# Hyena short convolution in a two-layer encoder kernel: shifted products by ScalarE activations and accumulating DMAs in place of VectorE

## Chip, cores and metric

The kernel runs on one core of one Trainium2 chip. The metric is device time in microseconds (us) of one execution. The core's engines are PE (TensorE; its weight loads are listed apart as PEld), DVE (VectorE), ACT (ScalarE), POOL (GpSimd) and SP (SyncE, which only issues DMAs here). POOL issues DMAs too.

## Reference

A trunk of two layers on 1024 tokens of 1024 channels, all in float32. Layer 0 mixes tokens by attention and RWKV-7, layer 1 by a bidirectional Hyena operator, and each layer ends with a gated feed-forward network. The change lies in the Hyena operator:

```
p = h @ w_in                                        # [1024, 3 * 1024]
p = conv_general_dilated(p, conv_w, width 3, centred, one filter per channel) + conv_b
v, x1, x2 = jnp.split(p, 3, axis=-1)
z = v
for o, gate in enumerate((x1, x2)):
    z = gate * bidirectional_fft_conv(z, filt[:, o, 0], filt[:, o, 1], skip[o])
return z @ w_out
```

The width-3 convolution is, for each channel, `w0 * p[t-1] + w1 * p[t] + w2 * p[t+1] + b`.

## The kernel before, in words

Channels lie on the 128 partitions and tokens along the free dimension. SBUF is cut into pages of 128 x 1024 float32 (called p in the profile), PSUM into eight banks of 128 x 512 (bk). Pages and banks are taken and given back while the program is written down, the oldest free one first, so taking a page means waiting for its last users.

The Hyena layer runs two chains side by side.

The **front** (`front`, `finish`) makes 24 tiles of 128 channels, in four pieces of six: two tiles of v, two of x1, two of x2. For each tile `proj_steps` multiplies by weights that POOL's queue loads one tile ahead (`load_w`, L271, two DMAs of 512 KB from the DRAM tiles hwi..., into pages that the tile before the last has to release): 48 products of 128x512 on PE (L296, float32 as pairs of two parts) into two banks. `padded` (L1033 to L1036) copies the banks to a page with a zero column at each end; POOL sets the zeros and ACT copies. `hy_short` then makes the convolution: ACT writes o = w1 * pad[1:1025] + b (L1818), DVE adds w0 * pad[0:1024] (L1819) and w2 * pad[2:1026] (L1820). For v and x1 `hy_tok` transposes o on PE (L1831) and ACT copies the transposes out (L1832); x2 is stored to DRAM by SP (sp_h).

The **back** (`back`) takes the pieces in turn. `start` makes the first transform of v on PE (L1770, "sums"), and ACT evicts it (L1771). `hy_conv` is a long run of DVE work: a transform (`dft8`, L1648 and L1649), products with the filters' spectra (L1794 to L1798, spectra loaded by SP, L1793), sums (L1804, L1805) and a transform back. `gate` then multiplies back on PE (L1923), DVE multiplies by x1 (L1928), and PE makes the next transform (L1780, "taps"), evicted by ACT (L1698) and combined by DVE (L1699, L1700). A second `hy_conv` follows, with the sums of the next piece inside it, and `finals` (PE L1946, DVE L1950) ends the piece. Behind the front's last tile the output projection of the first four results (`tail`, L296 and L787) runs beside the back.

`weave` puts the two chains into one program in proportion to given costs, and the framework's scheduler then sets each engine's order. An engine works through its order one by one, so an instruction that waits holds up all behind it.

Of the kernel before, what the change touches and what calls it, by code (L numbers as in the profile page):

```python
# [32 lines left out]
def rows(ap):  # L33
    """[n*128] (or [a, n*128]) vector -> [rows, 128]."""
    if len(ap.shape) == 2:
        return ap.rearrange("a (r w) -> (a r) w", w=P)
    return ap.rearrange("(r w) -> r w", w=P)
# [9 lines left out]
def weave(*gens):  # L47
    """Runs generators of steps side by side, in proportion to their lengths: (n, generator). A step counts for what it
    yields, or for one; one that yields "wait" has to wait for the others."""
# [19 lines left out]
def some(gen, n):  # L69
    """The next n steps of a generator."""  # L70
    for _ in range(n):
        if next(gen, gen) is gen:
            return
        yield


class Kern:
    """The kernel's shared state and building blocks.

    SBUF is cut into pages and PSUM into banks, handed out and taken back while the program is traced: the oldest  # L80
    free one first, so that reuse waits as little as it can. Pages are for float32 ([128, 1040]) or for float32r
    operands of products ([128, 1024]); repage() cuts the free ones anew between the parts of the program.
    """

# [32 lines left out]
    def fence(self, dt, n=1 << 30, first=0):  # L117
        """Only the pages from `first` up to the n-th are for common use."""
# [11 lines left out]
    def repage(self, nf, nr):  # L130
        """Cuts the pages into nf of float32 and nr of float32r; those in use stay."""
# [36 lines left out]
    def set_banks(self, *counts):  # L168
        """Splits the (free) banks into groups."""
# [23 lines left out]
    def small(self, tag, shape, bufs, dt=F32):  # L193
        """One of `bufs` small tiles in turn; the caller sees to it that an older use has ended by then."""
# [20 lines left out]
    def load_cols(self, spec):  # L215
        """spec: list of (key, AP [rows, width] or tuple of APs set side by side); a row becomes a column. Steps of 128."""
# [42 lines left out]
    def split(self, t, shape=(P, 1024)):  # L259
        """The pair of a page, which is given back."""  # L260
        hi, lo = self.page(shape, F32R), self.page(shape, F32R)
        self.split_into(hi, lo, t)
        self.free(t)
        return hi, lo

    def load_w(self, ap, kt, ncol):
        """ap: DRAM [kt*128, ncol] -> (hi, lo), [128, kt, ncol] each; ap may also be what presplit() returned."""
# [9 lines left out]
    def presplit(self, ap, kt, ncol, name):  # L277
        """The pair of load_w() as DRAM tiles."""
# [7 lines left out]
    def mm3(self, ps, w, mov, first=True, last=True, halves=(0, 1)):  # L286
        """ps[n] = sum_k w[k]^T mov[k][:, n-th half]; pairs (hi, lo) of [128, M] and [128, 1024]. The first and last
        addends may be left to other calls."""
# [9 lines left out]
    def proj_steps(self, w, c0, width, h, g=0, ahead=None, n=4, apart=False):  # L298
        """proj_tile() in n steps; the halves one after the other if `apart`."""
# [15 lines left out]
    def stream(self, w, h, tiles, g=0):  # L315
        """Projections one after another, each one's `post` beside the next: (column, width, post), post(banks) a generator."""
        late = iter(())
        n = 4
# [17 lines left out]
    def proj_tile(self, w, c0, width, h, g=0, ahead=None):  # L336
        """w[:, c0:c0+width]^T h in two banks; a column in `ahead` is that of the next call, whose weights are loaded here."""
# [33 lines left out]
    def ada_first(self):  # L371
        """Layer 0's first two sixths, by the tensor engine."""
# [19 lines left out]
    def ada_cols(self, layer, part, half, acc, g):  # L392
        """The columns of half a sixth from rows to be summed."""
# [13 lines left out]
    def ada_part(self, layer, part, g=0, lag=0):  # L407
        """Modulation columns of one sixth: [128, 8] at self.mod[:, layer*48 + part*8]. The last product of a half comes
        `lag` steps after its sums."""
# [35 lines left out]
    def rstd(self, acc, n):  # L445
        """1/sqrt(mean_D(x^2) + eps) on all partitions, [128, 512] of a half in PSUM; acc holds sums of squares."""
# [12 lines left out]
    def normed(self, xT, steps, use, lag, keep=None):  # L459
        """use(n, m, r) for the halves n of the tiles m of x, r the bank of rstd(); `steps` yields (n, m) as they get done,  # L460
        half 0 first. A tile that is done goes to the tile `keep` in DRAM. Half 0 is used beside the steps of half 1, from
        its step `lag` on."""
# [31 lines left out]
    def inv_sqrt(self, out, ps, mult, add=None, floor=None):  # L494
        """out = 1/sqrt(ps*mult + add) or 1/sqrt(max(ps, floor))."""
# [8 lines left out]
    def norm_h(self, xT, layer, which, steps, lag, keep=None):  # L504
        """rmsnorm(x)*gain*(1+scale)+shift as pairs of [128 channels, 1024 tokens]; for the rest see normed()."""
# [23 lines left out]
    def head_cols(self, sq, g):  # L529
        """sq [128 = 2 heads x 64, 1024 tokens] -> bank [128 tokens, 8 blocks, 2 heads] of sums."""  # L530
# [5 lines left out]
    def head_bcast(self, cols, n, g):  # L536
        """cols [128 tokens, 8, 2 heads] -> bank [128 = 2 heads x 64, 512] of token half n."""
# [7 lines left out]
    def to_tok(self, out, src, g):  # L545
        """src [128 channels, 1024 tokens] -> out [128 tokens, 8 blocks, 128 channels]."""
# [9 lines left out]
    # The up-projections multiply blocks of 2 x 2 (two tiles of outputs, halves of the channels, halves of the tokens)  # L556
    # with seven products, Winograd's form of Strassen's: with C = A B,
# [1619 lines left out]
```

## Time and profile before

| | us |
|---|---|
| median of 3 timed runs | 3468.43 |
| lowest and highest of them | 3458.44, 3473.36 |
| span of the profiled execution, which is one by itself | 3477.4 |
| Hyena layer in it, first L1818 to the end of the last L1950 | 2187.1 to 2736.6 |

The profiled execution's own time is known as its span, from the first instruction to the last. Busy time of an engine is the time in which it worked on an instruction; a timeline merges instructions of one line and gives start, length, count, and in square brackets the idle time ahead with what ended it. Times in timelines and stretches count from the start of the span.

### The profile page before, as it was taken

The page shows a single profiled execution, that of the slowest core. Times are in us where ns is not written, and L with a number is a line of the kernel's source. Part 1 is how long each engine was busy: PE and PEld are TensorE (multiplying, and loading weights), DVE is VectorE, ACT ScalarE, POOL GpSimd, SP SyncE. Part 2 cuts the span into 40 slices and gives each one's busy share as a digit, 9 for nine tenths or more (in the row PEclk, how much of TensorE's full clock was granted, in tenths as well). Part 3 has the DMA queues.
Part 4 walks back from the last instruction along what each step waited for, and adds up shares of the span by engine and source line. Part 5 has one row for each costly group of instructions (what it writes and reads, how often), then busy time and mean ns, then how long its engine had stood idle before and what let it go on. Part 6 is the DMA issues. An engine that isn't in the chain of part 4 may idle for free.

```text
span 3477.4 us, 52810 instructions
## 1 busy us (share of the span) xinstructions
PE 3277.4 (94%) x20739; PEld 2639.1 (76%) x20739; DVE 2355.9 (68%) x4281; ACT 1255.1 (36%) x2296; POOL 240.6 (7%) x502
## 2 busy tenths in 40 slices
PE   8999989999998998999999999989987799999998
PEld 4577766777677887887788887778876688888887
DVE  5345556566667778587777666589987786667545
ACT  4523245556543543342223333321221153333211
POOL 2000000000011231000000220000000000000000
PEclk9789989999998999999999999999998899999999
DMA  7454523333324326234444994324336523223411
GB/s 261 172 164 148 159 84 75 73 96 82 73 63 105 99 77 213 79 127 151 158 147 135 359 356 160 103 81 144 121 104 228 177 74 108 73 73 129 146 53 49
DMA packets 332536, 458.89 MB, mean 132 GB/s; under 512 B 103992, under 2 KB 234897, under 8 KB 332288
## 3 DMA queue, kind: packets, MB, share of 16 engines
q1 hardware_dynamic: 292576, 321.65, 30.1%
q0 software_dynamic: 39536, 133.81, 11.3%
q8 instruction: 163, 2.67, 0.3%
q14 instruction: 85, 0.70, 0.1%
q10 hardware_dynamic: 176, 0.07, 0.0%
HBM read 311.27 MB, written 141.56 MB: 130 GB/s over the span
## 4 chain that ended last, share of the span: by engine, by line
PE 60%; DVE 9%; DMA 5%; issue 4%; ACT 2%; SPq 0%; POOL 0%; DVEq 0%; ACTq 0%; POOLq 0%
PE bk L296 22%; PE bk L600 7%; PE bk L602 7%; PE bk L601 7%; PE bk L1749 4%; PE bk L1735 2%; PE bk L1770 2%; DMA p<-in_ada_w_dram 2%; DVE p L1648 1%; DVE p L257 1%; PE bk L1263 1%; PE bk L1327 1%; PE bk L947 1%; DMA p<-in_hy_w_in_dram 1%; PE bk L964 1%
## 5 line engine op out<-in xcount | busy, mean ns | idle before, releaser
L296 PE MATMUL bk<-p,p 128*128 128x512 f32 (+1 forms) x5136 | 1252.3, 403 | 66.9 <-ACT p L256 26.4
L296 PEld LDWEIGHTS bk<-p,p 128*128 128x128 f32 (+1 forms) x5136 | 979.5, 193 | 304.4 <-ACT p L256 30.1
L256 ACT ACTIVATE p<-p 128x512 fp32r<-128x512 f32 (+3 forms) x534 | 395.8, 759 | 930.3 <-PE bk L601 260.6
L257 DVE TENSOR_TENSOR p<-p,p 128x512 fp32r<-128x512 f32 (+3 forms) x534 | 443.5, 848 | 225.3 <-ACT p L256 183.6
L601 PE MATMUL bk<-p,p 128*128 128x512 f32 x1248 | 488.3, 392 | 3.8 <-DVE p L257 3.8
L600 PE MATMUL bk<-p,p 128*128 128x512 f32 x1248 | 488.4, 393 | 0.0
L602 PE MATMUL bk<-p,p 128*128 128x512 f32 x1248 | 487.6, 392 | 0.2 <-DVE p L257 0.2
L601 PEld LDWEIGHTS bk<-p,p 128*128 128x128 f32 x1248 | 236.3, 189 | 53.4 <-DVE p L257 4.7
L602 PEld LDWEIGHTS bk<-p,p 128*128 128x128 f32 x1248 | 236.2, 189 | 50.4 <-DVE p L257 0.8
L600 PEld LDWEIGHTS bk<-p,p 128*128 128x128 f32 x1248 | 236.1, 189 | 48.9
L787 DVE SCALAR_TENSOR_TENSOR p<-bk,mod,p 128x512 f32<-128x512 f32 x192 | 135.0, 745 | 119.8 <-PE bk L296 116.6
L1648 DVE TENSOR_TENSOR p<-p 128x128 f32<-128x128 f32 (+2 forms) x544 | 174.0, 383 | 0.0
L429 DVE SCALAR_TENSOR_TENSOR p<-p,cond,p 128x512 f32<-128x512 f32 x140 | 104.5, 748 | 82.7 <-DMA p<-in_ada_w_dram 81.0
L1749 PE MATMUL bk<-p,p 128*128 128x128 f32 x1024 | 137.0, 290 | 2.7 <-DVE p L1700 2.6
L1749 PEld LDWEIGHTS bk<-p,p 128*128 128x128 f32 x1024 | 126.5, 201 | 7.9 <-ACT p L1737 2.4
L928 DVE TENSOR_REDUCE mx<-bk 128x1 f32<-128x512 f32 x128 | 86.9, 685 | 61.8 <-PE bk L925 58.8
L1737 ACT ACTIVATE p<-delta,k_tneg 128x128 f32<-128x128 f32 x256 | 87.9, 394 | 84.0 <-DMA hs<-p 14.0
L1036 ACT COPY p<-bk 128x512 f32<-128x512 f32 (+1 forms) x80 | 44.0, 589 | 197.3 <-DVE p L1797 64.3
L948 ACT COPY p<-bk 128x512 f32<-128x512 f32 x128 | 74.4, 588 | 105.3 <-PE bk L947 100.7
L932 ACT ACTIVATE p<-bk,mx 128x512 f32<-128x512 f32 x128 | 87.0, 686 | 29.4 <-DVE mx L929 29.0
L947 PE MATMUL bk<-k_ident,p 128*128 128x128 f32 x512 | 85.0, 294 | 10.8 <-ACT p L932 9.3
L1327 PEld LDWEIGHTS bk<-p,p 64*64 64x64 f32 x2048 | 73.0, 137 | 28.9 <-issue 17.6
(404 smaller groups left out, 4373.4 us busy)
## 6 DMA issues: line engine op xcount, KB each, us to landing
p<-in_ffn_w_dram SPq DMA_DIRECT2D x120, 512.0 KB, 4.5
p<-in_ada_w_dram SPq DMA_DIRECT2D x96, 512.0 KB, 4.5
sp_f<-p POOLq DMA_DIRECT2D x36, 512.0 KB, 5.5
p<-sp_f POOLq DMA_DIRECT2D x36, 512.0 KB, 5.4
hs<-p POOLq DMA_DIRECT2D x64, 256.0 KB, 3.1
p<-hs SPq DMA_DIRECT2D x32, 512.0 KB, 4.2
p<-sp_r SPq DMA_DIRECT2D x24, 512.0 KB, 5.6
p<-sp_x SPq DMA_DIRECT2D x24, 512.0 KB, 4.5
```

Of the source, the lines that this page charges most:

```text
L256: self.nc.scalar.activation(out=hi, in_=src, func=AF.Copy)
L257: self.nc.vector.tensor_tensor(out=lo, in0=src, in1=hi.bitcast(F32), op=ALU.subtract)
L296: nc.tensor.matmul(ps[n], a, b[:, HALVES[n]], start=s, stop=e)
L429: nc.vector.scalar_tensor_tensor(out=acc, in0=wt[:, i], scalar=self.cond[:, k : k + 1], in1=acc, op0=ALU.mult, op1=ALU.add)
L600: nc.tensor.matmul(ps, op[:, 0, k], mh, start=start and k == 0, stop=False)
L601: nc.tensor.matmul(ps, op[:, 0, k], ml, start=False, stop=False)
L602: nc.tensor.matmul(ps, op[:, 1, k], mh, start=False, stop=stop and k == 3)
L787: nc.vector.scalar_tensor_tensor(out=xs, in0=ps[n], scalar=self.modc(layer, part, m), in1=xs, op0=ALU.mult, op1=ALU.add)
L947: nc.tensor.transpose(pt[:, j], pr[:, k * P : (k + 1) * P], self.ident)
L1327: nc.tensor.matmul(pt[H[p], pr], lhs(e, pr, p), rhs[H[p], 8 * e + pr], start=True, stop=True)
L1648: tt = lambda o, a, b, op: nc.vector.tensor_tensor(out=o, in0=a, in1=b, op=op)
L1749: nc.tensor.matmul(ps[:, j, ri], F[2 * d + t2 // 4][:, t2 % 4, 128 * ri : 128 * ri + 128], tp[:, j, d], start=d == 0, stop=d == 1)
```

## The change

ACT makes all three scaled copies, into three pages. POOL then issues two DMAs from page to page that add to what the destination holds: first the copy scaled by w0 into o, then the copy scaled by w2. A tile takes two pages more, each for a short while. Only `hy_short` differs; other lines move by four numbers (L1831 becomes L1835, L1923 L1927, L1946 L1950).

```diff
     def hy_short(self, pad, j):
         nc = self.nc
-        o = self.page()
+        o, a = self.page(), self.page()
         cw = lambda a: self.c("conv_w", 24 * a + j)
         nc.scalar.activation(out=o, in_=pad[:, 1:1025], func=AF.Identity, scale=cw(1), bias=self.c("conv_b", j))
-        nc.vector.scalar_tensor_tensor(out=o, in0=pad[:, 0:1024], scalar=cw(0), in1=o, op0=ALU.mult, op1=ALU.add)
-        nc.vector.scalar_tensor_tensor(out=o, in0=pad[:, 2:1026], scalar=cw(2), in1=o, op0=ALU.mult, op1=ALU.add)
-        self.free(pad)
+        nc.scalar.activation(out=a, in_=pad[:, 0:1024], func=AF.Identity, scale=cw(0))
+        nc.gpsimd.dma_start(out=o, in_=a, accum_op=ALU.add)
+        self.free(a)
+        a = self.page()
+        nc.scalar.activation(out=a, in_=pad[:, 2:1026], func=AF.Identity, scale=cw(2))
+        nc.gpsimd.dma_start(out=o, in_=a, accum_op=ALU.add)
+        self.free(a, pad)
         return o
```

The scheduler's orders differ from the first tile on. Three places show how. In all of them p_ and a number is a page, bk_ a bank.

POOL at the start of the layer, before: loads of weights (hwi), one pair of DMAs for each tile, with one pad's zero column between them.

```order
L271 DMA p_238<-hwi8h 128x1024
L271 DMA p_11467<-hwi8l 128x1024
L271 DMA p_11455<-hwi9h 128x1024
L271 DMA p_11483<-hwi9l 128x1024
L1034 MEMSET p_86 128x1
L271 DMA p_238<-hwi16h 128x1024
L271 DMA p_11467<-hwi16l 128x1024
```

POOL at the same place with the change, from the load of hwi9 on:

```order
L271 DMA p_11483<-hwi9l 128x1024
L1820 DMA p_106<-p_94 128x1024
L1034 MEMSET p_86 128x1
L1820 DMA p_90<-p_16650 128x1024
L1824 DMA p_106<-p_102 128x1024
L1824 DMA p_90<-p_16654 128x1024
L271 DMA p_238<-hwi16h 128x1024
L271 DMA p_11467<-hwi16l 128x1024
L1033 MEMSET p_106 128x1
L1820 DMA p_16662<-p_16666 128x1024
L1824 DMA p_16662<-p_16670 128x1024
L271 DMA p_11455<-hwi17h 128x1024
```

The weight loads and the pads' zeros now stand behind the accumulating DMAs of earlier tiles, and each L1824 has to wait for the L1820 into the same page.

ACT at the first two tiles, before: pad copies, one activation for each tile, then copies of transposes.

```order
L1036 COPY p_86<-bk_66 128x512
L1036 COPY p_94<-bk_68 128x512
L1818 ACTIVATE p_106<-p_86,cols 128x1024
L1818 ACTIVATE p_130<-p_94,cols 128x1024
L1832 COPY p_102<-bk_69 128x4x128
```

ACT at the same place with the change:

```order
L1036 COPY p_86<-bk_66 128x512
L1036 COPY p_98<-bk_68 128x512
L1818 ACTIVATE p_106<-p_86,cols 128x1024
L1819 ACTIVATE p_94<-p_86,cols 128x1024
L1823 ACTIVATE p_102<-p_86,cols 128x1024
L1818 ACTIVATE p_90<-p_98,cols 128x1024
L1819 ACTIVATE p_16650<-p_98,cols 128x1024
L1823 ACTIVATE p_16654<-p_98,cols 128x1024
L1036 COPY p_16658<-bk_63 128x512
```

Each tile has three activations in a row, and the copies of transposes come after the next tile's pad copies.

PE inside the first gate, before (L1923 gate products, L1780 taps, L296 projection products):

```order
L1780 MATMUL bk_64<-p_94,p_122 128x256 x2
L1923 MATMUL bk_70<-p_130,p_118 128x256 x2
L1923 MATMUL bk_70<-p_130,p_126 128x256 x2
L296 MATMUL bk_66<-p_11495,p_11467 128x512
L1923 MATMUL bk_67<-p_16654,p_118 128x256 x2
L1923 MATMUL bk_67<-p_16654,p_126 128x256 x2
L1780 MATMUL bk_64<-p_94,p_122 128x256 x2
```

PE inside the first gate with the change:

```order
L1780 MATMUL bk_64<-p_90,p_122 128x256 x2
L1927 MATMUL bk_70<-p_16678,p_118 128x256 x2
L1927 MATMUL bk_70<-p_16678,p_126 128x256 x2
L296 MATMUL bk_68<-p_11491,p_11455 128x512
L296 MATMUL bk_69<-p_242,p_11455 128x512
L296 MATMUL bk_68<-p_242,p_11455 128x512
L296 MATMUL bk_69<-p_11491,p_11483 128x512
L296 MATMUL bk_68<-p_11491,p_11483 128x512
L296 MATMUL bk_69<-p_11475,p_11455 128x512
L296 MATMUL bk_68<-p_11475,p_11455 128x512
L1927 MATMUL bk_67<-p_16698,p_118 128x256 x2
```

More projection products stand inside the gate. Over the first gate there are 78 of them where there were 50, over the third none where there were 24, and over the fourth 109 where there were 81. Counted from the first product of the third tile, 286, 600, 912 and 1128 projection products stood ahead of the four gates, and 246, 542, 912 and 1056 stand there now; 1272 stand ahead of the end of the last piece in both. Of the transposes of the first two tiles the change's order puts both behind the 48 products of the third tile, where they stood behind 29 and 72.

## Rows read from the trace of the kernel before

**Rows 1.** Page, part 1: engine, busy us (share of the span), instructions.
```profile
PE 3277.4 (94%) x20739; PEld 2639.1 (76%) x20739; DVE 2355.9 (68%) x4281; ACT 1255.1 (36%) x2296; POOL 240.6 (7%) x502
```
**Rows 2.** Stretches of the Hyena layer: busy time of each engine in each.
```profile
core 0: us, PE busy (x) PEld busy (x) DVE busy (x) ACT busy (x) POOL busy (x), PEclk, DMA share, GB/s
2216.00:2600.00 384.00, 354.25 (x1656) 298.11 (x1655) 338.33 (x591) 87.67 (x133) 22.94 (x65) 0.96 0.33 108
...
2276.00:2400.00 124.00, 113.92 (x535) 96.13 (x534) 108.98 (x183) 26.74 (x40) 8.52 (x25) 0.94 0.36 119
2400.00:2520.00 120.00, 113.35 (x541) 95.93 (x540) 112.32 (x200) 25.21 (x38) 7.26 (x21) 0.97 0.35 114
2520.00:2645.00 125.00, 97.33 (x445) 79.92 (x444) 113.81 (x195) 26.82 (x39) 6.87 (x17) 0.89 0.43 146
2645.00:2737.00 92.00, 66.35 (x282) 54.93 (x281) 69.55 (x128) 4.35 (x6) 4.25 (x8) 0.83 0.61 207
```
**Rows 3.** PE timeline: third tile's start, a run of projection products, the four gates' first products.
```profile
2191.58 8.48 PE L296 MATMUL bk<-p,p 128*128 128x512 f32 x29 [4.99 <-DMA p<-hwi8h]
...
2250.72 25.23 PE L296 MATMUL bk<-p,p 128*128 128x512 f32 x110
2275.78 1.89 PE L1923 MATMUL bk<-p,p 128*128 128x256 f32 x8
...
2400.39 1.89 PE L1923 MATMUL bk<-p,p 128*128 128x256 f32 x8
...
2520.12 1.89 PE L1923 MATMUL bk<-p,p 128*128 128x256 f32 x8
...
2644.56 1.89 PE L1923 MATMUL bk<-p,p 128*128 128x256 f32 x8
```
**Rows 4.** DVE timeline: the last piece's gated products.
```profile
2732.21 4.37 DVE L1950 TENSOR_TENSOR p<-p,bk 128x512 f32<-128x512 f32 x4 [3.39 <-PE bk L1946]
```
**Rows 5.** Stretches of DVE convolution work, instructions of L1819 alone: busy time (count).
```profile
2229.00:2276.00 47.00, 3.80 (x3) 1.00 0.41 135
2303.00:2404.00 101.00, 7.67 (x6) 0.93 0.36 121
2424.00:2523.00 99.00, 6.39 (x5) 0.97 0.37 121
2544.00:2647.00 103.00, 5.09 (x4) 0.87 0.45 157
```
**Rows 6.** Groups by line (busy us, mean ns), and the view of line L1818.
```profile
L1819 DVE SCALAR_TENSOR_TENSOR p<-p,cols,p 128x1024 f32<-128x1024 f32 x24 | 30.6, 1277 | 20.5 <-issue 14.2 <-ACT p L1818 6.3
...
L1818 ACT ACTIVATE p<-p,cols x24: 1237/1246/1262, 2187.1 to 2614.3; 128x1024 f32<-128x1024 f32 x24
```
**Rows 7.** DMA issues, median us to landing; then weight loads of L271, 2186:2600 and 2180:2680.
```profile
p<-p SPq DMA_DIRECT2D x10, 256.0 KB, 3.2
...
sp_f<-p POOLq DMA_DIRECT2D x36, 512.0 KB, 5.5
...
DMA to landing us min/median/max: 3.5/4.3/8.8
...
DMA to landing us min/median/max: 3.5/4.6/17.0
```
**Rows 8.** A weight load's issue on POOL (ns), and POOL's waits, 2186:2600 (total, times, longest).
```profile
L271 POOL DMA_DIRECT2D p<-hwi16h x1: 536/536/536, 2205.2 to 2205.2; - x1
...
POOL p L271 <- PE bk L296: 237.4, 23, 29.4
```
**Rows 9.** Waits of ScalarE for VectorE and of VectorE for ScalarE, 2186:2600.
```profile
ACT p L1036 <- DVE p L1797: 64.3, 5, 14.4
...
DVE p L1699 <- ACT p L1698: 15.8, 6, 5.9
```
**Rows 10.** ACT timeline at the first two tiles: last pad copies, then L1818 of both.
```profile
2186.18 1.07 ACT L1036 COPY p<-bk 128x512 f32<-128x512 f32 x2 [0.28 <-PE bk L296]
2187.14 2.38 ACT L1818 ACTIVATE p<-p,cols 128x1024 f32<-128x1024 f32 x2
```

## Prediction

> **What bounds the kernel now.** I read the views in this order. First the page's busy times: PE is busy 94% of the span and DVE 68%, so PE looks like the only limit [rows 1]. That share is an average, so next I cut the only place that the change touches, the Hyena layer, into stretches. There DVE is no longer at 68%: between 2276 and 2645 us it is busy 109.0 of 124, 112.3 of 120 and 113.8 of 125 us, beside PE at 113.9, 113.4 and 97.3 [rows 2]. Two engines share the limit. ScalarE is at about 26 us in each of these stretches and has room [rows 2].
>
> The PE timeline says how the stretches hang together. The gates (the products of L1923 between a piece's two convolutions) start at 2275.8, 2400.4, 2520.1 and 2644.6 us [rows 3]. The DVE timeline gives the end of the loop: the last gated product begins at 2732.2 and runs 4.4 [rows 4]. A gate needs the finished convolution from DVE, and the next convolution needs the gate from PE. What the change can win is thus won from gate to gate, and only where DVE, not PE, is late.
>
> **What is removed.** 48 VectorE passes, 24 of L1819 at 30.6 us together [rows 6] and 24 of L1820 of the same shape, 61.2 in all. What matters is where they stand: by stretches L1819 takes 3.80, 7.67, 6.39 and 5.09 us (3, 6, 5 and 4 times), and L1820, right behind it, the same [rows 5]. So 7.6, 15.3, 12.8 and 10.2 us leave the four DVE stretches ahead of the four gates; the rest lies where DVE waits.
>
> **What is added.** ScalarE: 48 more activations of the form of L1818, at 1246 ns: 59.8 us [rows 6], beside 26 us busy per 120; its busy time hides, its place in the queue is costed below. POOL: 48 more issues at 0.54 us, the duration of a weight load's issue [rows 8], 26 us; covered by the 237 us that POOL spends waiting for PE before it may load weights [rows 8]. If that cover went, weight loads would be late, which is a rival below.
>
> The transfers themselves are not in the trace: an addition into a page in SBUF. Call one's time to landing X. Below, a copy from page to page of half the bytes lands in 3.2 us; above, the slowest weight load on POOL's queue took 17.0 [rows 7]. Nearest is the plain 512 KB store that POOL issues, 5.5 [rows 7]; an addition has to read its destination too, so I take X = 6 and keep 3.2 and 17.0 for the range.
>
> The Trainium skill ("Collectives: The Full Stack", section "The bandwidth ceiling: the fold count and why AG ≠ RS ≠ AR") says that a transfer that adds runs at about half the rate of a copy, for its two reads, not for the addition. No run here shows it yet. By it X would be an estimate of up to 11, twice the 5.5, and the sum below would come to about 3464, by the later start alone.
>
> **The wait that is added.** The second transfer of a tile adds into the same page, so POOL waits X at L1824, and what is queued behind it there is the next tile's weight load and pad memset. A tile is ready 1.1 (pad copies) + 2.4 (two activations) [rows 10] + 2X + 0.5 after its products, 16 us at X = 6, where it was 1.1 + 3 times 1.2 = 4.7 before. In the changed order the transposes stand later to match. At the start: the first two tiles' activations begin at 2187.1 [rows 10], and by the same steps the last of the four transfers is issued at 2199.7 and lands at 2205.7; PE, which begins the third projection at 2191.6 [rows 3], ends it 48 products later at 2202.6 and waits 3 us. But 37 products now stand between these transposes and the sums where there were 63 with the transposes in two places, so the sums start near 2216, as they did. At X = 3.2 nothing changes, at X = 17.0 the start is 21 us later. I cost it at zero.
>
> **The sum, gate by gate.** A projection product takes 25.23 / 110 = 0.229 us [rows 3]. Counted in the two orders from the third projection on, 286, 600, 912 and 1128 products stood before the four gates; now it is 246, 542, 912 and 1056, with 1272 at the end in both.
> To gate 1: DVE loses 7.6, and 40 fewer products stand ahead (9.2 us of PE): −7.6.
> Gate 1 to 2, 124.6 us: DVE loses 15.3, but 28 more products stand inside the gate (78, not 50), where DVE has to wait: +6.4. Together −8.9.
> Gate 2 to 3, 119.7 us: PE is busy 113.4 [rows 2] and gets 58 more products, +13.3, which makes 126.7. PE sets this one: +7.0, and DVE's 12.8 is worth nothing.
> Gate 3 to 4, 124.5 us: DVE loses 10.2, and the 24 products inside the gate move out, −5.5: −15.7. PE has 72 products fewer here.
> Gate 4 to the end of the last gated product, 92 us: no short convolution is left here; 28 more products stand inside the gate: +6.4. The products behind it, some 24 us, lie under DVE's work on the last convolution.
> That is −18.8. Against it: in the gates ScalarE evicts the taps (L1698) for DVE, which already waited 15.8 us for it [rows 9]; two more activations may now stand ahead, up to 2.4 us in each of four gates, 9.6 in all. PE's products pace part of the gates anyway, so I take half, +4.8. The total is −14. The tail behind the layer is the same program. The profiled execution had a span of 3477.4, which would become 3463.4. It lies 9.0 us over the median of the timed runs, 3468.43, and is not among them; against that median the forecast is **3454 us**.
>
> **Rivals.**
> (a) Slower: POOL's queue becomes the bound. Per tile it issues two loads (1.1), waits for ScalarE (3.5), for the first transfer (X) and issues two transfers (1.1): 5.7 + X, against 427.2 / 23 = 18.6 us from tile to tile between the first L1818 and the last [rows 6]. From X = 12.9 on every tile is late: weights land late and PE stops at L296. At X = 17.0 it is 4.1 times 24, 98 us, and 21 at the start, less the 19 won: **3568**. For it: the slowest load, and two pages more per tile in a pool where ScalarE already waited 64.3 us in five waits for pages that DVE had still to release [rows 9]. Against it: on that queue, beside DVE busy 338 of 384 us [rows 2], the loads landed in 3.5 to 8.8, median 4.3 [rows 7].
> The Trainium skill ("SBUF — State Buffer", section "SBUF: two separate sides") warns of this: transfers issued by GpSimd stall while VectorE holds the port that they share, in some of its modes, since the descriptors cannot be written. By that rule X would be long here and the time that of (a); the trace disagrees so far with its loads of 4.3 median, so its chance is inside that of (a).
> (b) Faster: all of DVE's 45.9 us come off, PE's heavier third stretch filling gaps instead of setting the pace; less the 4.8: **3427**. For it: PE has 70 us idle from 2276 to 2737 [rows 2]. Against it: the first three stretches have PE at over 90%.
> (c) Nothing: the −32 of the DVE-bound terms are eaten by pages and by ScalarE's queue: **3468**.
> (d) Slower in another place: ScalarE's three activations in a row delay evictions, and PE lacks banks. 59.8 us of work, two thirds of it on the path, 40, against the 14 won: **3494**. It decides where PE's waits for ScalarE grow beyond the 14 us won. Against it: ScalarE's load stays under 40% in each stretch.
>
> **How the numbers follow.** Half a per cent is 17 us, about what a measurement of this kernel can tell from no change. The forecast has 0.43, of which 0.15 lies under 3451, since X and the gates may both turn out better; (b) 0.17, (c) 0.16, (a) 0.13, (d) 0.11. Faster: 0.15 + 0.17 = 0.32. Same: 0.28 + 0.16 = 0.44. Slower: 0.13 + 0.11 = 0.24. The range takes in (b) to (d), 3426 to 3494, and leaves out (a) and little else. The forecast's own range, by friction from 0 to 9.6 and a start up to 10 us later, is 3449 to 3469.
>
> **What would show it.** Right: DVE's busy time 61 us lower and ScalarE's 60 higher; L1820 and L1824 landing near 6 us; gates at about 2268, 2384, 2511 and 2619, and the last gated product over near 2718 to 2723, if the profile's span starts alike. The third step should be the longest of the three, with PE nearly full. Wrong: a landing above 12.9 us, PE waiting at L296 for weights or at L1835 for transfers, or gates more than 10 us from these times.

## The result: slower by a quarter of a per cent, and the profile after

The changed kernel takes 3484.24 us (median of 14 runs, 3474.08 to 3488.63), the kernel before 3473.53 us beside it (14 runs): a ratio of 1.0026, 95% interval 1.0016 to 1.0036, about 9 us. The forecast was 3454 us, 14 us faster. The time lies in the range, which was wide enough for a loss (3426 to 3494), and within 0.5% of no change, but the sign was wrong: the relief came, and something larger came with it.

Page, part 1, of the kernel after (engine, busy us, share of the span, instructions):

```profile
span 3476.2 us, 52930 instructions
...
PE 3269.3 (94%) x20739; PEld 2634.3 (76%) x20739; DVE 2297.9 (66%) x4233; ACT 1304.9 (38%) x2344; POOL 282.6 (8%) x550
```

Against [rows 1], DVE is 58 us lower and ACT 50 us higher, near the 61 and 60 forecast, and POOL 42 us higher, where 26 were forecast. The profiled execution took 3477.93 us, 6 under the median, so it shows places rather than the exact size. The stretches, with the same cuts as the last four of [rows 2], and one more from the second gate to the third:

```profile
core 0: us, PE busy (x) PEld busy (x) DVE busy (x) ACT busy (x) POOL busy (x), PEclk, DMA share, GB/s
2276.00:2400.00 124.00, 108.32 (x508) 91.06 (x506) 94.46 (x177) 41.66 (x53) 18.94 (x36) 0.93 0.60 155
2400.00:2520.00 120.00, 115.73 (x561) 97.78 (x559) 95.97 (x180) 38.81 (x52) 20.23 (x35) 1.00 0.68 183
2520.00:2645.00 125.00, 87.36 (x399) 73.40 (x400) 101.70 (x187) 36.99 (x48) 15.14 (x27) 0.84 0.68 193
2645.00:2737.00 92.00, 71.70 (x325) 59.72 (x324) 65.75 (x114) 4.40 (x6) 4.30 (x8) 0.87 0.62 217
2391.00:2515.00 124.00, 123.30 (x597) 104.44 (x596) 99.03 (x190) 38.60 (x51) 21.49 (x37) 1.00 0.70 185
```

DVE is down to 94 to 102 us in each of the first three, where it had 109 to 114, so it is no longer what fills them. But PE did not fill up in its place: it has 108 of 124 and 87 of 125 us in the first and third, less than before. The PE timeline names a new wait (start, length, and in brackets the idle time ahead with its releaser), with the third tile's start and the first products of the four gates as in [rows 3]:

```profile
2186.99 12.55 PE L296 MATMUL bk<-p,p 128*128 128x512 f32 x48 [4.63 <-DMA p<-hwi8h]
...
2263.62 1.89 PE L1927 MATMUL bk<-p,p 128*128 128x256 f32 x8
...
2304.43 1.09 PE L1835 MATMUL bk<-k_ident,p 128*128 128x128 f32 x4 [6.22 <-DMA p<-p]
...
2328.42 1.94 PE L1835 MATMUL bk<-k_ident,p 128*128 128x128 f32 x8 [8.11 <-DMA p<-p]
...
2391.08 1.89 PE L1927 MATMUL bk<-p,p 128*128 128x256 f32 x8
...
2514.54 1.89 PE L1927 MATMUL bk<-p,p 128*128 128x256 f32 x8
2524.19 1.94 PE L1835 MATMUL bk<-k_ident,p 128*128 128x128 f32 x8 [7.76 <-DMA p<-p]
...
2630.62 3.52 PE L1927 MATMUL bk<-p,p 128*128 128x256 f32 x8 [23.20 <-DVE p L1648]
```

PE stops at the transposes (L1835) of a tile until the transfer into it (`DMA p<-p`, page to page) has landed, three times for 22.1 us together. (The longest wait of all, 23.20 us for DVE ahead of the fourth gate, is not the transfers' doing: without them it is 22.55, in e1_no_dma below.) Where such a wait falls between a gate's products, DVE stops with PE; its timeline right behind the third of these waits:

```profile
2528.85 0.75 DVE L1932 TENSOR_TENSOR p<-p,bk 128x256 f32<-128x256 f32 x2 [8.88 <-PE bk L1927]
```

How a tile comes to be late shows ahead of the second of these waits, the one of 8.11 us. ACT and POOL, from their timelines:

```profile
2310.94 0.59 ACT L1036 COPY p<-bk 128x512 f32<-128x512 f32 x1 [4.80 <-DVE p L1648]
2311.56 1.25 ACT L1818 ACTIVATE p<-p,cols 128x1024 f32<-128x1024 f32 x1
...
2316.20 1.13 ACT L1819 ACTIVATE p<-p,cols 128x1024 f32<-128x1024 f32 x1
2317.24 1.14 ACT L1823 ACTIVATE p<-p,cols 128x1024 f32<-128x1024 f32 x1
```

```profile
2317.64 0.88 POOL L1820 DMA_DIRECT2D p<-p  x1 [4.72 <-ACT p L1819]
...
2322.46 0.88 POOL L1824 DMA_DIRECT2D p<-p  x1 [1.00 <-DMA p<-p]
```

The pad copy waits for a page that DVE (L1648) releases, the activations follow it, the first addition waits for them (L1820), the second for the first (L1824), and PE goes on 6 us behind the second's issue.

The additions themselves, in the view of the DMA issues, have a median landing of 5.6 us; the views of L1820 and then of L1824 give their issue on POOL (ns) and the spread:

```profile
p<-p POOLq DMA_DIRECT2D x48, 512.0 KB, 5.6
```

```profile
L1820 POOL DMA_DIRECT2D p<-p x24: 847/876/1267, 2185.5 to 2617.2; - x24
...
DMA to landing us min/median/max: 4.5/6.0/19.2
```

```profile
L1824 POOL DMA_DIRECT2D p<-p x24: 847/868/884, 2194.7 to 2636.9; - x24
...
DMA to landing us min/median/max: 4.5/5.5/9.4
```

And the waits of POOL and ScalarE that come with them, from 2150 to 2760 us (total, times, longest):

```profile
POOL p L1824 <- DMA p<-p: 78.6, 13, 18.9
...
ACT p L1036 <- DMA p<-p: 27.9, 6, 8.5
```

The second addition of a tile waits for the first (L1824), and pad copies (L1036) wait for pages that the copies still hold until they have landed.

### The profile page after: what moved, and what is told of

Its sections match the earlier page's. It is cut to its first block, busy times and chain, and to the rows that moved or that the text cites. A ratio compares the mean times of both kernels' runs of the same rounds, so it can differ in the third digit from the quotient of the medians.

```text
span 3476.2 us, 52930 instructions
## 1 busy us (share of the span) xinstructions
PE 3269.3 (94%) x20739; PEld 2634.3 (76%) x20739; DVE 2297.9 (66%) x4233; ACT 1304.9 (38%) x2344; POOL 282.6 (8%) x550
## 3 DMA queue, kind: packets, MB, share of 16 engines
q0 software_dynamic: 46448, 158.98, 15.3%
## 4 chain that ended last, share of the span: by engine, by line
PE 55%; DVE 11%; DMA 6%; issue 5%; ACT 2%; POOL 1%; SPq 0%; DVEq 0%; POOLq 0%; ACTq 0%
PE bk L296 17%; PE bk L600 7%; PE bk L602 7%; PE bk L601 7%; PE bk L1749 3%; DVE p L1648 2%; PE bk L1735 2%; DMA p<-in_ffn_w_dram 2%; DVE p L257 1%; DMA p<-p 1%; PE bk L1263 1%; DMA p<-in_ada_w_dram 1%; PE bk L1770 1%; PE bk L1327 1%; PE bk L947 1%
## 5 line engine op out<-in xcount | busy, mean ns | idle before, releaser
L296 PE MATMUL bk<-p,p 128*128 128x512 f32 (+1 forms) x5136 | 1244.6, 401 | 38.5 <-DVE p L787 12.8
L296 PEld LDWEIGHTS bk<-p,p 128*128 128x128 f32 (+1 forms) x5136 | 973.9, 192 | 270.7 <-issue 15.9
L1648 DVE TENSOR_TENSOR p<-p 128x128 f32<-128x128 f32 (+2 forms) x544 | 173.6, 383 | 0.0
L1737 ACT ACTIVATE p<-delta,k_tneg 128x128 f32<-128x128 f32 x256 | 87.8, 394 | 86.0 <-DMA hs<-p 13.4
L1036 ACT COPY p<-bk 128x512 f32<-128x512 f32 (+1 forms) x80 | 44.3, 589 | 154.4 <-PE bk L296 58.3
L1699 DVE TENSOR_TENSOR p<-p,bk 128x256 f32<-128x256 f32 (+1 forms) x80 | 37.6, 470 | 89.7 <-ACT p L1698 69.5
L478 ACT ACTIVATE p<-p 128x512 f32<-128x512 f32 x80 | 49.8, 633 | 123.8 <-DVE p L814 116.0
```

Source lines behind the costliest of these rows:

```text
L296: nc.tensor.matmul(ps[n], a, b[:, HALVES[n]], start=s, stop=e)
L1648: tt = lambda o, a, b, op: nc.vector.tensor_tensor(out=o, in0=a, in1=b, op=op)
L1737: nc.scalar.activation(out=tp[:, j, d], in_=delta, func=AF.Exp, scale=tneg[:, 8 * d + t2 : 8 * d + t2 + 1])
```

## The experiments

Theory L: a tile is late by two landings in series, and PE, which works in a fixed order, waits at its transposes. Rivals: S, ScalarE's longer queue and the pages for the copies; O, PE's new order of work; Q, GpSimd's queue, where weight loads and pad memsets stand behind the additions; and traffic, 24 MB more on the DMA engines. Each ratio below is to the kernel before, timed beside it. Where two kernels' orders on PE are set side by side, the number is that of places, out of the 20739 matmuls of the program, at which another source line stands.

**e1_no_dma**

```diff
         nc.scalar.activation(out=a, in_=pad[:, 0:1024], func=AF.Identity, scale=cw(0))
-        nc.gpsimd.dma_start(out=o, in_=a, accum_op=ALU.add)
...
-        nc.gpsimd.dma_start(out=o, in_=a, accum_op=ALU.add)
```

> Both accumulating transfers are left out; the three activations and their pages stay. The output lacks the two outer taps of the short convolution. Theory L (the two transfers in series keep the tile back, and PE waits for it at the transposes): the 22 us of waiting at L1835 go, and the 14 us forecast at first come out: about 3455 to 3462 beside 3474 for the kernel before. Theory S (ScalarE's longer queue and the pages for the copies): the transfers are nothing, it stays at 3480 to 3486. Theory O (PE and its order set the time, and VectorE's time is worth nothing here): 3470 to 3477.

Measured: 3451.01 us, ratio 0.9932 [0.9916, 0.9948], 4 us below the range of L and outside those of S and O. Without the transfers the same copies are 23 us faster than before, so the transfers cost the change about 33 us. (PE's order moves with them: e1_no_dma differs from the change in 491 places.) Of the PE's idle time at the transposes 9.1 us are left, where the change has 25.2 and the kernel before 19.4 (groups by line from 2150 to 2790 us; busy, mean ns, idle):

```profile
L1833 PE MATMUL bk<-k_ident,p 128*128 128x128 f32 x128 | 18.1, 281 | 9.1 <-ACT p L1036 7.3 <-ACT p L1818 1.9
```

```profile
L1835 PE MATMUL bk<-k_ident,p 128*128 128x128 f32 x128 | 20.1, 305 | 25.2 <-DMA p<-p 22.1 <-ACT p L1836 1.6 <-ACT p L1036 0.9
```

```profile
L1831 PE MATMUL bk<-k_ident,p 128*128 128x128 f32 x128 | 20.1, 303 | 19.4 <-ACT p L1036 19.4
```

The first of these is of e1_no_dma, the second of the change, the third of the kernel before. The wait ahead of the fourth gate stays in e1_no_dma:

```profile
2605.54 3.78 PE L1925 MATMUL bk<-p,p 128*128 128x256 f32 x8 [22.55 <-DVE p L1648]
```

**e2_centre**

```diff
         nc.scalar.activation(out=o, in_=pad[:, 1:1025], func=AF.Identity, scale=cw(1), bias=self.c("conv_b", j))
-        nc.scalar.activation(out=a, in_=pad[:, 0:1024], func=AF.Identity, scale=cw(0))
...
-        nc.scalar.activation(out=a, in_=pad[:, 2:1026], func=AF.Identity, scale=cw(2))
```

> Only the activation of the centre tap is left; neither VectorE passes nor further activations nor transfers. The output lacks the two outer taps. It is what taking 61 us off VectorE can bring at most. Theory L: within 4 us of the run without transfers. Theory S: at least 10 us less than that run, about 3455 to 3462 where that run is at 3480 to 3486. Theory O: 3470 to 3477, like the kernel before.

Measured: 3457.31 us, 0.9948 [0.9932, 0.9964], not faster than e1_no_dma; 6 us above it by the medians, where L allowed 4, with intervals that overlap. ScalarE's 48 extra copies and their pages cost nothing that can be told: S falls. The two do not share PE's order (808 places differ), and e2_centre, whose order is nearer to the kernel before, is fast with PE idle at the transposes as long as before, 19.4 us:

```profile
L1829 PE MATMUL bk<-k_ident,p 128*128 128x128 f32 x128 | 20.1, 297 | 21.3 <-ACT p L1036 19.5 <-ACT p L1818 1.8
```

**e3_one_dma**

```diff
-        nc.scalar.activation(out=a, in_=pad[:, 0:1024], func=AF.Identity, scale=cw(0))
-        nc.gpsimd.dma_start(out=o, in_=a, accum_op=ALU.add)
...
+        nc.vector.scalar_tensor_tensor(out=o, in0=pad[:, 0:1024], scalar=cw(0), in1=o, op0=ALU.mult, op1=ALU.add)
```

> Half the change: VectorE adds the left tap, one activation and one accumulating transfer make the right one. Theory L: one landing of 6 us less on each tile, so most of the waiting at L1835 goes, while half of VectorE's gain stays: 3464 to 3472. Theory S: half of the loss, 3477 to 3481. Theory O: 3472 to 3478.

Measured: 3480.43 us, 1.0026 [1.0012, 1.0039], the same as with two transfers: a miss for L (3464 to 3472), in the range of S. PE waits little for transfers at the transposes here:

```profile
L1832 PE MATMUL bk<-k_ident,p 128*128 128x128 f32 x128 | 20.0, 303 | 18.6 <-ACT p L1036 15.3 <-DMA p<-p 3.2
```

Taken alone this says little, since DVE has 24 passes back; e14_tap_no_dma takes it apart.

**e4_x2_dma**

```diff
-        o, a = self.page(), self.page()
+        o = self.page()
...
+        if j < 16:
+            nc.vector.scalar_tensor_tensor(out=o, in0=pad[:, 0:1024], scalar=cw(0), in1=o, op0=ALU.mult, op1=ALU.add)
+            nc.vector.scalar_tensor_tensor(out=o, in0=pad[:, 2:1026], scalar=cw(2), in1=o, op0=ALU.mult, op1=ALU.add)
+            self.free(pad)
+            return o
+        a = self.page()
```

> The change for the x2 tiles alone, 8 of 24, which are stored and not transposed; v and x1 keep VectorE. Theory L: no transposed tile waits for a transfer, 20 us leave VectorE: 3464 to 3470, faster than both kernels. Theory S: a third of the loss, 3476 to 3479. Theory O: 3472 to 3476.

Measured: 3472.93 us, 0.9995 [0.9979, 1.0010], a miss for L (3464 to 3470), in the range of O. x2 tiles go to DRAM and nobody waits for them, and the loss is gone; but the expected gain of some us isn't there either.

**e5_scratch_pool, e6_scratch_sp**

```diff
-        nc.gpsimd.dma_start(out=o, in_=a, accum_op=ALU.add)
+        nc.gpsimd.dma_start(out=self.dram(f"sa{j}"), in_=a)      # e6: nc.sync
...
+        nc.gpsimd.dma_start(out=self.dram(f"sb{j}"), in_=a)      # e6: nc.sync
```

> Leaves out the two outer taps: the same 48 transfers of 512 KB are issued by GpSimd at the same places, but as plain stores into DRAM tiles that nobody reads, so the tile does not wait for them. What stays: GpSimd's 48 issues and its waits for ScalarE, the pages of the copies held until a transfer lands, the bytes. What goes: the landing in front of the transposes, GpSimd's wait for the first landing, and the program order of PE goes back to that of the kernel without transfers (3451). Landing theory (the tile is late by two landings in series): 3448 to 3456. Queue theory (weight loads and pad memsets stand behind the transfers on GpSimd): 3460 to 3475, since the waits for ScalarE stay, with PE waiting at L296 or ScalarE at L1036. Traffic theory (24 MB more on the DMA engines slow other transfers): 3470 to 3484.

> As the one before, with the plain stores issued by SyncE instead of GpSimd, so that GpSimd's queue is as it was without transfers. Landing theory: 3448 to 3456, like the one before. Queue theory: 3448 to 3456, and at least 8 us below the one before. Traffic theory: 3470 to 3484, like the one before.

Measured: from GpSimd 3459.58 us, 0.9949 [0.9930, 0.9968], between the ranges of L and Q; from SyncE 3451.66 us, 0.9927 [0.9912, 0.9943]. The same number of bytes, though into DRAM and without the sum, costs nothing when no tile waits for it: the traffic theory falls as far as this tests it. GpSimd's queue may cost up to the 8 us between the two (the intervals overlap). The other 25 or so go with the landing in the tile.

**e7_weights_on_sp**

```diff
             for t, d in zip(out, ap):
-                self.nc.gpsimd.dma_start(out=t.rearrange("p k n -> p (k n)"), in_=d)
+                o = t.rearrange("p k n -> p (k n)")
+                if getattr(self, "wq", None):                                   # nc.sync in the Hyena projections alone
+                    self.wq.dma_start(out=o.bitcast(F32), in_=d.bitcast(F32))
...
```

> The whole change, with the loads of the Hyena projection weights moved from GpSimd to SyncE, so that they no longer stand behind GpSimd's waits for the transfers. The order of PE is that of the changed kernel nearly to the row. Queue theory: 3455 to 3470, and the waits of PE at the transposes for transfers go from 22 us to under 10. Landing theory: 3478 to 3488, the waits at the transposes stay. Order theory (the framework's scheduler lays PE's work out otherwise because it plans with the transfers, and that layout costs the time): 3478 to 3488.

Measured: 3483.92 us, 1.0022 [1.0007, 1.0037]; PE's waits at the transposes for transfers are 28.0 us. Taking the weight loads out from behind the additions changes nothing: Q falls as far as it speaks of the loads.

**e8_late_transposes**

```diff
-            for _ in range(4):
+            for _ in range(8):
                 yield
```

> The whole change, with the use of a tile put eight projection steps behind its activations instead of four, so that another 11 us of PE's own work stand between the additions and the transposes. Landing theory: the waits of PE at the transposes for transfers (22 us) go to under 5, and the time falls to 3460 to 3470; it need not reach 3451, since the first sums of the layer start up to 8 us later. Queue theory: 3475 to 3488. Order theory: another layout, no forecast nearer than 3460 to 3495, but then without a link to the waits at the transposes.

Measured: 3486.57 us, 1.0032 [1.0018, 1.0046], a miss for L, in the range of Q. PE's wait at the transposes for transfers is gone, as L said, but the time isn't:

```profile
L1835 PE MATMUL bk<-k_ident,p 128*128 128x128 f32 x128 | 18.6, 286 | 13.4 <-ACT p L1036 12.9 <-issue 0.5
```

Two waits of e8 from 2150 to 2760 us that have grown:

```profile
ACT p L1036 <- DMA p<-p: 50.2, 7, 15.8
...
PE bk L296 <- ACT p L256: 40.0, 3, 25.7
```

The first, pad copies that wait for pages, was 27.9 in the change, and the second 1.8. One wait was traded for others, and the edit moved more of the program than it was meant to (PE's order differs from the change's in 1244 places), so it decides little; but it shows that PE's waits at the transposes are not the only way in which the transfers cost time.

**e9_copy_sp, e10_small, e16_copy_gpsimd**

```diff
-        nc.gpsimd.dma_start(out=o, in_=a, accum_op=ALU.add)
+        nc.sync.dma_start(out=o, in_=a)                                          # e9
+        nc.gpsimd.dma_start(out=o[:, 0:8], in_=a[:, 0:8], accum_op=ALU.add)      # e10
+        nc.gpsimd.dma_start(out=o, in_=a)                                        # e16
```

> Leaves out the sum: each transfer of the change is a plain copy of the same 512 KB into the tile itself, issued by SyncE, so the last tap alone is left. Against the plain stores by SyncE into tiles that nobody reads (3451.7) it differs in one thing: the transfers land in the tile, so the second waits for the first and the transposes and stores of the tile wait for both, and the framework's scheduler lays PE's work out for that, as in the changed kernel. GpSimd's queue and the addition are out. Landing theory: 3472 to 3486, with PE's waits at the transposes for transfers at 15 us or more. If the cost were GpSimd's queue or the addition (its second read): 3450 to 3460.

> Leaves out the outer taps but for 8 of 1024 columns: the same 48 accumulating transfers from GpSimd, in the same places and with the same dependences, of 4 KB instead of 512 KB. They should land in some 2 us instead of 5.6. Landing theory: the cost goes with the time to landing in series, so 33 us times 2/5.6 at most: 3451 to 3464, and PE's waits at the transposes for transfers under 8 us. Order theory (the layout of PE's work that the scheduler makes for kernels with these dependences costs the time, not the landing): 3472 to 3486, since the dependences are the same and the transposes stand nearly as late as with the whole transfers.

> Leaves out the sum: the transfers of the change as plain copies into the tile, from GpSimd, so that the last tap alone is left. Against the change it lacks the addition alone; against the plain copies by SyncE (ratio 0.9970, landing 3.4 us) it has GpSimd's queue. If the addition makes the landing long: landing 3.4 to 4.5 us and a ratio of 0.996 to 0.999. If GpSimd's queue does: landing 5 us or more, as with the addition, and 1.001 to 1.004.

Measured: e9 3469.44 us, 0.9970 [0.9957, 0.9984], landing 3.4 us; e10 3458.18 us, 0.9947 [0.9928, 0.9967], landing 2.1; e16 3464.15 us, 0.9977 [0.9962, 0.9991], landing 4.3. e10 is in the range of L, e16 in that of a landing made long by the addition; e9 is 3 us under L's, with 7.3 us of waits for transfers where 15 were expected. Each keeps the two transfers in series and the waits for them; what differs is the time to landing, and in e9 and e16 also the issue (by SyncE in e9; 0.53 us on GpSimd in e16, against 0.87 in e10 and the change). PE's order is nearly that of the change (it differs in 322 places in e10, 36 in e9 and 2 in e16), so O falls. In e16 VectorE and ScalarE follow the change's order throughout. With the orders held, a landing of 4.3 us in place of 5.6 is worth 0.0049, 17 us; that the shorter issue is not what does it shows in e10, which has the long one and is as fast as e5 without any landing in the tile. The three groups at the transposes, in the order e10, e9, e16:

```profile
L1835 PE MATMUL bk<-k_ident,p 128*128 128x128 f32 x128 | 18.1, 282 | 10.1 <-ACT p L1036 8.0 <-DVE p L1796 1.4 <-DMA p<-p 0.8
```

```profile
L1835 PE MATMUL bk<-k_ident,p 128*128 128x128 f32 x128 | 18.6, 291 | 14.6 <-DMA p<-p 7.3 <-ACT p L1036 7.0 <-issue 0.3
```

```profile
L1835 PE MATMUL bk<-k_ident,p 128*128 128x128 f32 x128 | 18.5, 291 | 17.3 <-DMA p<-p 16.4 <-ACT p L1036 0.5 <-issue 0.3
```

**e13_halves**

```diff
-        nc.gpsimd.dma_start(out=o, in_=a, accum_op=ALU.add)
+        for n in range(2):
+            nc.gpsimd.dma_start(out=o[:, HALVES[n]], in_=a[:, HALVES[n]], accum_op=ALU.add)
```

> The whole change, each addition cut into two transfers of 256 KB by halves of the tokens, so that the second copy's first half waits for the first copy's first half alone. Landing theory: the time from the first issue to the last landing of a tile falls from 11 us to 7 to 9, though GpSimd issues 48 more transfers of 0.87 us. At 7.8 us of time per us of landing (from the runs with 2.1 and 5.6 us) that is worth up to 15 us: 3466 to 3482. If only the bytes or the issues count: 3484 or more.

Measured: 3478.56 us, 1.0009 [0.9995, 1.0023], in the range of L, but its interval overlaps that of the change, and PE's idle time at the transposes is no shorter in its profile (26.9 us): inconclusive. A half lands in 4.8 us, not half of 5.6:

```profile
p<-p POOLq DMA_DIRECT2D x96, 256.0 KB, 4.8
```

**e14_tap_no_dma**

```diff
-        nc.gpsimd.dma_start(out=o, in_=a, accum_op=ALU.add)      # from e3_one_dma
```

> Leaves out the right tap: the kernel with one transfer (ratio 1.0026 to the kernel before) without that transfer; ScalarE makes the copy, VectorE adds the left tap. It prices one landing on its own. If each landing costs alike, one costs half of the two's 0.0094, and this kernel comes to 0.998, 3469. If the first landing behind a tile costs most of it, because what counts is whether the tile comes after the transposes' place or not, this comes to 0.993 to 0.996, 3452 to 3462.

Measured: 3476.65 us, 1.0001 [0.9989, 1.0013], above both ranges. One landing by itself thus costs 0.0025, 9 us (1.0026 of e3 less 1.0001), by the medians less than half of two, though the intervals leave room for half. What I hadn't expected is that one tap off DVE is worth nothing, and both are worth 0.7%. PE still waits 15.3 us at the transposes for pad copies there, near the 19.4 of before and not the 9.1 of e1. By itself that can't be the reason, since e2 is fast with 21.3. What stands out in its profile is that the projection products wait for ScalarE's copies of transposes (L1832), 18.6 us, where e2 has 3.5:

```profile
L296 PE MATMUL bk<-p,p 128*128 128x512 f32 x1554 | 384.5, 404 | 64.6 <-ACT p L256 29.0 <-ACT p L1832 18.6 <-DVE p L787 8.5
```

Whether that costs the gain was not tried and stays open; S is refuted for the kernels without a DVE tap, not for this one.

**e15_three**

```diff
+        a = self.page()
+        nc.scalar.activation(out=a, in_=pad[:, 2:1026], func=AF.Identity, scale=cw(2))
+        nc.gpsimd.dma_start(out=o, in_=a, accum_op=ALU.add)
```

> The change with a third transfer: the right tap is made and added twice (so it counts double). Landing theory: a third landing of 5.6 us in series; at 33 us for two it adds 15 to 45 us: 3499 to 3530, and PE's waits at the transposes for transfers go well above 22 us. If the additions are hidden but for the first: 3484 to 3490.

Measured: 3522.53 us, 1.0131 [1.0114, 1.0149], in the range of L: a third landing costs another 0.0105, 37 us. The transposes' group:

```profile
L1839 PE MATMUL bk<-k_ident,p 128*128 128x128 f32 x128 | 22.2, 324 | 39.9 <-DMA p<-p 38.7 <-ACT p L1036 1.2
```

**e11_gpsimd_adds, e12_x2_gpsimd_adds**

```diff
-        nc.gpsimd.dma_start(out=o, in_=a, accum_op=ALU.add)
+        nc.gpsimd.tensor_tensor(out=o, in0=o, in1=a, op=ALU.add)      # e12: for j >= 16 alone, VectorE for the rest
```

> A version that might beat both: the same three copies by ScalarE, summed by GpSimd's own tensor additions instead of by transfers. There is no landing; a row of this kernel for such an addition on GpSimd is missing, so by the nearest row, VectorE's 1.27 us per pass, two additions in series take from 2.5 us (as fast as VectorE) to 10 us (a quarter as fast). Landing theory: at 2.5 to 5 us in series, 3451 to 3466; at 10 us, about what two landings in series take, 3475 to 3490. If GpSimd's additions hold up VectorE, VectorE's mean times of other groups rise and the time is above 3484.

> As the one before, for the eight x2 tiles alone; v and x1 are summed by VectorE as before. The x2 tiles are stored and read back much later, so nobody waits for these sums, however long they take. 16 VectorE passes, 20 us, go; with transfers in their place (3472.9, against 3476.3 before) they brought nothing that the timing could tell. Landing theory: 3463 to 3474. If GpSimd's additions hold up VectorE: 3475 to 3490.

Measured: 3561.09 us, 1.0244 [1.0224, 1.0264], and 3490.46 us, 1.0040 [1.0024, 1.0055]. No landing, and e11 is still the slowest of all: PE waits 70.8 us at the transposes for GpSimd's additions, and these and DVE's passes are stretched beside each other (last section). e12 has e4's order on PE in every place, its sums are of x2 tiles alone, as e4's are, and it is 0.0045 slower than e4. No version with the whole sum beat the kernel before.

What the runs give together, by the time to landing into the tile (PE's idle time ahead of the transposes is that of their group from 2150 to 2790 us):

| kernel | landings in series | ratio | PE idle at transposes, us |
|---|---|---|---|
| e6, e5: none in the tile | 0 | 0.9927, 0.9949 | 10.6, 9.7 |
| e10: 4 KB | 2 x 2.1 us | 0.9947 | 10.1 |
| e9: copies, SyncE | 2 x 3.4 | 0.9970 | 14.6 |
| e16: copies, GpSimd | 2 x 4.3 | 0.9977 | 17.3 |
| the change | 2 x 5.6 | 1.0026 | 25.2 |
| e15 | 3 x 5.5 | 1.0131 | 39.9 |

Within these kernels time and idle time rise in step with the landing. Where PE's order is another, idle time at the transposes does not tell the time: 21.3 us in e2 at a ratio of 0.9948, 13.4 in e8 at 1.0032. About 16 of the change's 33 us stand at the transposes themselves (25.2 less 9.1). The two profiles, whose spans differ by 28.0 us, show a little more: PE waits 3.7 us longer at the taps (L1780, 5.4 against 1.7), and in the layer, from the first L1818 to the last gated product, it is 4 us longer busy with the same work (467.5 against 463.5), as products right behind a wait take longer: the 8 transposes at 2328.42 took 1.94 us, the 8 at 2233.22, without a wait, 1.05. The rest, with the pad copies that wait for pages, was not taken apart.

## Why the prediction was wrong, step by step

**The step that failed** is "In the changed order the transposes stand later to match ... I cost it at zero." It was worked out at the first two tiles, where it holds: there PE waits for no transfer at 2199 us, and gate 1 comes 76.6 us after the third tile's start (2263.62 less 2186.99) instead of 84.2, the −7.6 of the sum to a tenth. It was then taken for all 24 tiles. At the later ones pad copies wait for pages that DVE releases, the copies and both additions start late, and PE stands at the transposes: 25.2 us in the profile, 9.1 without the transfers. In all the transfers cost 33 us, where the step had zero. The agreement to a tenth is closer than one profile can bear: counted from the first L1818 (2187.14 before, 2182.91 now), gate 1 comes 7.9 us sooner. The prediction even listed PE waiting "at L1835 for transfers" as a sign that it would be wrong, without a price. X itself was right: 6 forecast, 5.5 to 6.0 measured.

**The other terms** (us), after and without the additions (e1_no_dma, gates at 2260.45, 2378.49, 2497.81 and 2605.54):

| term | forecast | after | e1 |
|---|---|---|---|
| gate 1 to 2, 124.6 before | −8.9 | +2.8 | −6.6 |
| gate 2 to 3, 119.7 | +7.0 | +3.7 | −0.4 |
| gate 3 to 4, 124.4 | −15.7 | −8.4 | −16.7 |
| gate 4 to the end, 92.0 | +6.4 | +12.2 | +9.0 |

Without the additions the signs hold but for a small one, and three of four terms come within 3 us. From gate 2 to 3 PE does set the pace in the change (123.30 of 124 us busy from 2391 to 2515), though the step was 3 us shorter than counted. The excess of the change over e1 in the first and third terms, 9.4 and 8.3 us, is about the waits that stand there: 8.11 at 2328 and 7.76 at 2524. The wait of 6.22 at 2304 has its like in e1 (6.95, for a pad copy), so it isn't the transfers' doing.

**ScalarE's friction**, +4.8, was too much for the copies alone: e1 against e2 shows no cost of them. DVE's wait for L1698 did grow, from 15.8 [rows 9] to 22.5 us from 2186 to 2600.

**The rivals.** (a) POOL's queue as the bound from X = 12.9 on: PE never waited long at L296 for weights, and e7 shows that the loads behind the additions don't matter; but the loss began far below 12.9, since what counts is when the tile is ready, not how many tiles POOL can serve. (b) All of DVE's work off the path would have been 3427; without the additions the kernel gains 23 us, between the forecast and (b). (c), no change, was near in time by the wrong cause: the relief was there, and was eaten by landings rather than by ScalarE's queue. (d) is the nearest in time on the slow side, 3494, but not by its mechanism: PE's waits for ScalarE, which were to grow, fell at the transposes from 19.4 to 2.5 us, and e1 with the same ScalarE work is fast.

The rule of the Trainium skill ("Collectives: The Full Stack", section "The bandwidth ceiling: the fold count and why AG ≠ RS ≠ AR"), that a transfer which adds runs at half the rate of a copy, is stated there for the steps of a ring of three ranks or more; the prediction carried it over to a single transfer. Here the same 512 KB from GpSimd landed in 4.3 us as a copy (e16) and in 5.6 as an addition, 1.3 times, in that direction but not twice.

## What to carry to other kernels

Here an operation moved from an engine to a transfer was paid for in the time to landing, again for each further transfer in a dependent chain, and in the end by the engine that works in order and stands at the consumer; bytes and the issuing queue cost little or nothing, and the landing still cost more than the engine time that it saves. Do the slack calculation for a late tile in the steady state, not for the first one, and price "engine X waits at the consumer" before it is called hidden. Where two landings in series can't be avoided, give them to the tiles that nobody waits for; here that took the loss away (e4) without a gain.

## What was not expected of the hardware

A transfer that adds holds GpSimd longer than one that copies: 0.87 us for an issue, of 512 KB and of 4 KB alike, against 0.53 for the copies of e16 (in e13 the halves of L1821 took 1.19 by the median, those of L1826 0.85). Half the bytes took 4.8 us to land and not 2.8, with two such transfers side by side; 4 KB took 2.1. An activation without a bias took 1.147 us (L1819), where L1818 with one takes 1.246 [rows 6]; the two also start at different columns, and no run tells the bias from that.

GpSimd's own addition of two 128 x 1024 pages takes 2.39 us by the median of 24 and 5.0 by the mean, with one of 36.8. Groups of e11_gpsimd_adds on the page, the view of L1820, and DVE's group L1796 from 2216 to 2737 us, which had 1214 ns in the change:

```profile
L1820 POOL TENSOR_TENSOR p<-p,p 128x1024 f32<-128x1024 f32 x24 | 120.1, 5006 | 68.8 <-ACT p L1819 50.6
```

```profile
L1820 POOL TENSOR_TENSOR p<-p,p x24: 2359/2392/36790, 2180.5 to 2688.1; 128x1024 f32<-128x1024 f32 x24
```

```profile
L1796 DVE TENSOR_TENSOR p<-p,p 128x1024 f32<-128x1024 f32 x28 | 37.7, 1372 | 0.0
```

The Trainium skill ("SBUF — State Buffer", section "SBUF: two separate sides") says that GpSimd and VectorE share a port pair, and that against a VectorE instruction with two SBUF inputs the one that starts first keeps it for the whole instruction; the stretched instructions on both engines agree, though no run tried it without the other engine. Its warning that transfers issued by GpSimd starve beside VectorE, in some of VectorE's modes, did not show: the longest issue of an addition at L1820 took 1.27 us. Whether VectorE ran in such a mode here the traces don't say. The slowest landing, 19.2 us, was that of the last x2 tile's L1820 at 2617.19, with eight weight loads issued on the same queue in the 13 us before.
